# A trunk kernel's recurrence stage: a temporary in another buffer, a scaling on another engine

## The chip, the cores and the metric

The kernel runs on one NeuronCore of a Trainium2 chip. The metric is the time of one execution on the device in microseconds. Five engines work side by side, each through its own list of instructions in order: TensorE (PE) multiplies, VectorE (DVE) and ScalarE (ACT) work element by element, GpSimd (POOL) does small steps, SyncE (SP) issues the loads of weights. They wait for each other by semaphores. SBUF is the memory on the core, PSUM the small one into which PE writes.

## What is computed

One layer of a trunk: x is 512 frames of 1024 channels, in float32. The part that matters here is the second of its two branches, a gated linear recurrence of 8 heads, and how it is normed and gated:

```python
def reference(x, w_in, ...):
    h = rmsnorm(x, norm_mix[l])
    proj = h @ w_in[l]
    zu, zv, zq, zf, zi, zo, g_a, g_b = jnp.split(proj, split_points, axis=-1)
    y_a = gmlp_branch(zu, zv, ...) @ w_up_a[l]
    y_b = hgrn2_branch(zq, zf, zi, zo, ..., hg_norm_g[l]) @ w_up_b[l]
    mix = jax.nn.sigmoid(g_a) * y_a + jax.nn.sigmoid(g_b) * y_b
    x = x + mix @ w_out[l]
    h = rmsnorm(x, norm_ffn[l])
    x = x + jnp.square(jax.nn.relu(h @ w_ff1[l])) @ w_ff2[l]
    return rmsnorm(x, final_norm)

def hgrn2_branch(zq, zf, zi, zo, lb, layer_idx, norm_g):
    log_f = jax.nn.log_sigmoid(zf32)
    k = jax.nn.sigmoid(-zf32)
    q = jax.nn.silu(zq)
    # S_t = diag(f_t) S_{t-1} + k_t v_t^T,  o_t = S_t^T q_t, per head
    o = hgrn2_chunkwise(q, k, zi, log_f)
    o = rmsnorm(o, norm_g) * jax.nn.silu(zo)     # norm over the 128 values of a head
    return o
```

## The kernel before

Frames and channels lie in tiles of 128 partitions. A float32 product is done as three matmuls: each operand is split into a high part H (the value rounded to the matmul's type, written by ACT, line 96) and a low part L (the rest, by DVE, line 97), and `mm3` (lines 120 to 122) adds H·H, H·L and L·H. Weights come in tiles of 128x1024 (`raw`, 4 buffers, loaded by SP); their split parts are WH and WL, 5 buffers each.

Two weight tiles for 256 channels are multiplied together by `seven`, a scheme of seven products in place of eight: it needs sums of the weight tiles, s1 to s4, in two tiles s12 and s34 (tag "S", 2 buffers, DVE, lines 148 to 156), which are split like any weight. Its products are named prodx and prodzy, its partial results u and u3. PE operands n1 to n4 are sums of frames prepared before.

The recurrence stage goes in four rounds of two heads. `gates_round` computes F, K and Q of a pair with `seven` (the query's silu by `fin_q`, with a temporary `sig` in pool pt). `hgrn_pair` then forms the scores within frames' cells: at each level b = 1, 2, 4, 8, 16, 32, 64 PE does many small matmuls (tile sp, line 455), DVE multiplies K and P by running products of F (T, `double`, line 481) and copies cells by a mask (line 488). `outputs` makes each head's result: transposes of K (pk, line 517), state products pst and st (lines 522 to 526), the outputs po in PSUM (lines 532 and 534), their squares summed by ACT (hjunk, line 536), rstd by two POOL steps (rs_h, rr_h, lines 226 and 228), and the scaled output o_n in SBUF by DVE (line 539), four tiles of 128 frames per head. po uses tag "hm", of which there are two buffers, so head h+1's po waits until the last buffer is read.

`gate_o(g)` computes the output gate of two heads: a projection acc, sg = sigmoid of it (ACT, line 555), sg = acc·sg and o_n = o_n·sg (DVE, lines 556 and 558). sg stands in a buffer of tag "S", the one of the sums. gate_o(0) to gate_o(2) follow rounds 1 to 3, gate_o(3) stands inside the merge gates that come after, which are eight further uses of `seven` (ga, and F, Q, V, K of the name "4"; their sigmoids on line 171).

At the end `onto_channels` transposes o_n (py, line 586), and ACT and DVE write it times the norm's weights hng as operands ybH and ybL (lines 588 and 589) for the projection with the weights "upb" (acc, lines 120 to 122 with 512 columns).

The order of instructions on each engine is not the order of the code: a scheduler with a cost model of its own places the whole program, subject to the buffers. So an edit to a buffer or an engine moves instructions on all engines around it.

Of the kernel before, what the change touches and what calls it, by code (L numbers as in the profile page):

```python
# [8 lines left out]
F32 = mybir.dt.float32  # L9
F32R = mybir.dt.float32r  # L10
I32 = mybir.dt.int32
AF = mybir.ActivationFunctionType
ALU = mybir.AluOpType
AX = mybir.AxisListType

P = 128
S = 512
# [56 lines left out]
def trunk_kernel(ctx: ExitStack, tc: tile.TileContext, A: dict, out: bass.AP):  # L74
    nc = tc.nc
# [4 lines left out]
    wp = ctx.enter_context(tc.tile_pool(name="wp", bufs=1))  # L80
# [140 lines left out]
    hng = cst.tile([P, 1], F32, name="hng")  # L221
# [37 lines left out]
    o_n = pr.tile([P, NT, D], F32, name="o_n")  # L259
# [102 lines left out]
    for t in range(NT):  # L362
# [4 lines left out]
        r = rstd_of(gp, mv[:, 1:2], 1, EPS, "l")  # L367
# [45 lines left out]
    pt = left3.enter_context(tc.tile_pool(name="pt", bufs=1, side="left", reuse_waits="tile"))  # L413
    left2 = ExitStack()
    hg = left2.enter_context(tc.tile_pool(name="hg", bufs=1, side="left", reuse_waits="tile"))
    ps_sc = left3.enter_context(tc.tile_pool(name="ps_sc", bufs=1, space=bass.MemoryType.PSUM))
    nc.sync.dma_start(hng, A["hg_norm_g"].rearrange("o v -> v o"))
    mask = {}
    for b in (0, *LEVELS):
        mask[b] = hg.tile([P, 16 if b else C], I32, name=f"mask{b}")  # L420
# [7 lines left out]
    def gates_round(r, V):  # L428
        F, K, Q = (held(n, r) for n in "FKQ")

        def fin_f(i, cols, src):
            nc.scalar.activation(K[:, i, cols], src, AF.Sigmoid, scale=1.0 if i else -1.0)
            nc.scalar.activation(F[:, i, cols], src, AF.Sigmoid, scale=-1.0 if i else 1.0)  # L433

        def fin_q(i, cols, src):
            qc = Q[:, i, cols]
            sig = pt.tile([P, S], F32, tag="sig", bufs=1, name="sig")[:, cols]
            nc.scalar.activation(sig, src, AF.Sigmoid, scale=-1.0 if i else 1.0)
            nc.vector.scalar_tensor_tensor(qc, src, -1.0 if i else 1.0, sig, ALU.mult, ALU.mult)

        for z, g, fin in ((ZF, F, fin_f), (ZQ, Q, fin_q)):
            seven(("chan", z + 256 * r), ("chan", z + 256 * r + 128), rhs, pt, ps_sc, g, fin, True)
        return V, F, K, Q

    def hgrn_pair(r, V, F, K, Q0):
        def flat(x):
            return x.rearrange("p h t -> p (h t)")

        def cellwise(sp, x, n, of=1):

            for h in range(2):
                for t in range(NT):
                    for p in range(0, NC, of):
                        c0 = t * P + p * C
                        nc.tensor.matmul(sp[p * C:(p + 1) * C, (h * NT + t) * n:(h * NT + t + 1) * n],  # L455
                                         K[:, h, c0:c0 + C], x(h, c0), start=True, stop=True)

        def bank(name):
            return ps_sc.tile([P, S], F32, tag="sp", bufs=2, name=f"sp{r}_{name}")


        sp = bank(0)
        cellwise(sp, lambda h, c0: Q0[:, h, c0:c0 + C], C)
        Q = held("P", r)
        nc.vector.tensor_tensor(flat(Q), flat(Q0), flat(F), ALU.mult)
        nc.vector.copy_predicated(cl.rearrange("p h t c -> p (h t) c"),
                                  mask[0][:, None, :].broadcast_to([P, 2 * NT, C]),
                                  sp[:, :2 * NT * C].rearrange("p (n c) -> p n c", c=C))


        T = flat(F)

        def double(b, T):

            n = 2 * S // (2 * b)
            T2 = T.rearrange("p (g i) -> p g i", i=2)
            Tn = hg.tile([P, n], F32, tag=f"T{b}", bufs=1, name=f"T{b}_{r}")
            nc.vector.tensor_tensor(Tn, T2[:, :, 0], T2[:, :, 1], ALU.mult)
            for x, i in ((K, 0), (Q, 1)):
                xv = flat(x).rearrange("p (g i b) -> p g i b", i=2, b=b)[:, :, i, :]  # L480
                nc.vector.tensor_tensor(xv, xv, T2[:, :, 1 - i, None].broadcast_to([P, n, b]), ALU.mult)
            return Tn

        for b in LEVELS:
            sp = bank(b)
            cellwise(sp, lambda h, c0: Q[:, h, c0:c0 + C].rearrange("p (g i b) -> p g i b", i=2, b=b)[:, :, 1, :], 16)
            T = double(b, T)
            nc.vector.copy_predicated(
                cl.rearrange("p h t (g i b) -> p (h t) g i b", i=2, b=b)[:, :, :, 1, :],
                mask[b][:, None, :].broadcast_to([P, 2 * NT, 16]).rearrange("p n (g b) -> p n g b", b=b),  # L490
                sp[:, :2 * NT * 16].rearrange("p (n g b) -> p n g b", n=2 * NT, b=b))
        for p in range(NC):
            nc.scalar.copy(sc[p * C:(p + 1) * C, :, :, p * C:(p + 1) * C], cl[p * C:(p + 1) * C])

        sp = bank(C)
        cellwise(sp, lambda h, c0: Q[:, h, c0 + C:c0 + 2 * C], C, 2)
        for p in range(0, NC, 2):
            nc.scalar.copy(sc[p * C:(p + 1) * C, :, :, (p + 1) * C:(p + 2) * C],
                           sp[p * C:(p + 1) * C, :2 * NT * C].rearrange("p (h t c) -> p h t c", h=2, t=NT))
        T = double(C, T)  # L500

        sp = bank(64)
        for h in range(2):
            for t in range(NT):
                nc.tensor.matmul(sp[0:64, (h * NT + t) * 64:(h * NT + t + 1) * 64], K[:, h, t * P:t * P + 64],
                                 Q[:, h, t * P + 64:(t + 1) * P], start=True, stop=True)
        nc.scalar.copy(sc[0:64, :, :, 64:128], sp[0:64].rearrange("p (h t c) -> p h t c", h=2, t=NT))
        T = double(64, T)
        for h in range(2):
            outputs(2 * r + h, V, K[:, h, :], Q[:, h, :], sc[:, h], T[:, h * NT:(h + 1) * NT])  # L510

    def outputs(h, V, K, Q, sc, Tt):
        hc = slice((h % 2) * P, (h % 2 + 1) * P)

        pk = ps.tile([P, NT, P], F32, tag="hm", bufs=2, name=f"pk{h}")
        for t in range(NT - 1):
            nc.tensor.transpose(pk[:, t, :], K[:, t * P:(t + 1) * P], ident)
        kd = hg.tile([P, NT - 1, P], F32, tag="kd", bufs=1, name=f"kd{h}")
        nc.scalar.copy(kd, pk[:, :NT - 1, :])
        pst = ps.tile([P, NT, P], F32, tag="hm", bufs=2, name=f"pst{h}")  # L520
        for t in range(NT - 1):
            nc.tensor.matmul(pst[:, t, :], kd[:, t, :], V[:, t, hc], start=True, stop=True)
        st = hg.tile([P, NT - 1, P], F32, tag="st", bufs=1, name=f"st{h}")
        nc.vector.tensor_copy(st[:, 0, :], pst[:, 0, :])
        for t in range(1, NT - 1):
            nc.vector.scalar_tensor_tensor(st[:, t, :], st[:, t - 1, :], Tt[:, t:t + 1], pst[:, t, :],
                                           ALU.mult, ALU.add)
        po = ps.tile([P, NT, P], F32, tag="hm", bufs=2, name=f"po{h}")
        ssq = hg.tile([P, NT], F32, tag="hssq", bufs=2, name=f"hssq{h}")
        junk = hg.tile([P, P], F32, tag="hjunk", bufs=2, name="hjunk")  # L530
        for t in range(NT):
            nc.tensor.matmul(po[:, t, :], sc[:, t, :], V[:, t, hc], start=True, stop=t == 0)
            if t:
                nc.tensor.matmul(po[:, t, :], Q[:, t * P:(t + 1) * P], st[:, t - 1, :],
                                 start=False, stop=True)
            nc.scalar.activation(junk, po[:, t, :], AF.Square, accum_out=ssq[:, t:t + 1])
        r = rstd_of(hg, ssq, NT, P * EPS, "h")
        for t in range(NT):
            nc.vector.tensor_scalar(o_n[:, t, h * P:(h + 1) * P], po[:, t, :], r[:, t:t + 1], P ** 0.5,
                                    ALU.mult, ALU.mult)  # L540

    def merge_gate(c0, d, g):
        seven(("chan", c0 + 128 * d), ("chan", c0 + 128 * d + 128), rhs, pt, ps_sc, g, act_by_sign(g, AF.Sigmoid), True)
# [7 lines left out]

    def gate_o(g):
        def evac_zo(tp, acc):
            sg = wp.tile([P, S], F32, tag="S", bufs=2, name="sg").rearrange("p (j c) -> p j c", j=2)
            nc.scalar.activation(sg, acc, AF.Sigmoid)
            nc.vector.tensor_tensor(sg, acc, sg, ALU.mult)
            ov = o_n[:, 2 * tp:2 * tp + 2, g * 256:(g + 1) * 256]
            nc.vector.tensor_tensor(ov, ov, sg, ALU.mult)

        tok_proj(ZO + 256 * g, evac_zo)  # L560
# [69 lines left out]
    for hf in range(2):  # L630
        W = [wload("out", hf, k) for k in range(4)]
        cs = slice(hf * 512, (hf + 1) * 512)
        for t in range(NT):
# [4 lines left out]
            junk = pn.tile([P, S], F32, tag="junk", bufs=1, name="junk")  # L638
# [56 lines left out]
    for t in range(NT):  # L695
        for hf in range(2):
            for f in range(NSLOW - 2, NSLOW):
                ff2(f, t, hf)
            c = x2[:, t, hf * S:(hf + 1) * S]
# [195 lines left out]
```

## Time and profile before

| what | value |
|---|---|
| three runs | 842.28, 842.15, 840.13 us, median 842.15 |
| profiled execution | 840.37 us |
| its span | 838.4 us |
| granted TensorE clock, mean | 0.985 |
| PE busy | 815.2 us (97%) |
| DVE busy | 607.4 us (72%) |
| ACT busy | 421.4 us (50%) |
| POOL busy | 50.6 us (6%) |

The span runs from the first to the last instruction of the profiled execution; its own time is 1.97 us longer. "Granted clock" is the share of full speed at which PE was allowed to run in a stretch; 1.00 stands for 2.4 GHz and 0.50 for 1.2 GHz. PE's busy time is that of instructions, at either speed. An idle time is put down to the instruction whose end released the waiting one.

### The profile page before, as it was taken

The numbers are of one execution on the slowest core, as the hardware profiler recorded it, in microseconds if no ns is written. First come the engines' busy times: TensorE is split into PE (matmuls) and PEld (weight loads), VectorE is DVE, ScalarE is ACT, GpSimd is POOL, SyncE is SP. The second block draws the span as 40 slices with busy tenths as digits, with TensorE's granted clock in tenths as the row PEclk, the third lists the DMA queues.
The fourth block names the chain that finished last, engine by engine and source line by source line (L and its number), as shares of the span: only waits on it lengthen the run. The fifth ranks groups of instructions, "written<-read, shape, count | busy, mean of one in ns | idle before, by whom it ended". The sixth has DMA issues, their size and how long they took to land.

```text
span 838.4 us, 16623 instructions
## 1 busy us (share of the span) xinstructions
PE 815.2 (97%) x7026; PEld 744.9 (89%) x7026; DVE 607.4 (72%) x829; ACT 421.4 (50%) x688; POOL 50.6 (6%) x79
## 2 busy tenths in 40 slices
PE   8999999989999999998999999999999999999996
PEld 7989899988999989998888889999999988778884
DVE  7775377946778589947565359887777575899996
ACT  6624364526437246544533332777767552555464
POOL 2010000000010100100000012000000000010103
PEclk9999999998999999998999999999999999999998
DMA  8242142311224013332533412233333396193812
GB/s 322 77 150 77 29 124 59 98 52 37 92 77 126 3 52 113 94 97 76 151 99 112 176 59 84 76 104 120 105 102 101 107 301 179 33 293 98 220 26 100
DMA packets 27212, 92.29 MB, mean 110 GB/s; under 512 B 4161, under 2 KB 4161, under 8 KB 27138
## 3 DMA queue, kind: packets, MB, share of 16 engines
q1 hardware_dynamic: 24834, 83.89, 31.1%
q0 software_dynamic: 1728, 6.29, 4.1%
q8 instruction: 55, 0.90, 0.4%
q10 hardware_dynamic: 576, 1.05, 0.3%
q14 instruction: 19, 0.16, 0.1%
HBM read 89.13 MB, written 2.10 MB: 109 GB/s over the span
## 4 chain that ended last, share of the span: by engine, by line
PE 92%; ACT 2%; DVE 2%; issue 1%; DMA 1%; POOL 1%; SPq 0%; POOLq 0%; ACTq 0%; DVEq 0%
PE acc L120 11%; PE acc L121 11%; PE acc L122 11%; PE prodx L120 7%; PE prodx L122 7%; PE prodx L121 7%; PE prodzy L120 5%; PE prodzy L122 5%; PE prodzy L121 5%; PE hm L121 3%; PE hm L120 3%; PE hm L122 3%; PE y L121 2%; PE y L120 2%; PE y L122 2%; PE sp L455 2%
## 5 line engine op out<-in xcount | busy, mean ns | idle before, releaser
L97 DVE TENSOR_TENSOR WL<-raw,WH 128x1024 fp32r<-128x1024 f32 (+1 forms) x134 | 147.3, 1104 | 87.9 <-ACT WH L96 87.3
L96 ACT ACTIVATE WH<-raw 128x1024 fp32r<-128x1024 f32 (+1 forms) x134 | 128.6, 963 | 141.3 <-PE prodx L121 29.2
L120 PE MATMUL acc<-WH,hTH 128*128 128x256 f32 x320 | 91.7, 287 | 1.1 <-ACT F L433 1.1
L122 PE MATMUL acc<-WH,hTL 128*128 128x256 f32 x320 | 90.8, 284 | 0.0
L121 PE MATMUL acc<-WL,hTH 128*128 128x256 f32 x320 | 90.3, 283 | 0.0
L97 DVE TENSOR_TENSOR WL<-s,WH 128x1024 fp32r<-128x1024 f32 x60 | 73.3, 1223 | 22.5 <-ACT WH L96 21.6
L96 ACT ACTIVATE WH<-s 128x1024 fp32r<-128x1024 f32 x60 | 63.6, 1061 | 40.1 <-PE prodzy L121 9.2
L120 PEld LDWEIGHTS acc<-WH,hTH 128*128 128x128 f32 x320 | 60.3, 189 | 1.7 <-ACT F L433 1.4
L121 PEld LDWEIGHTS acc<-WL,hTH 128*128 128x128 f32 x320 | 60.3, 188 | 0.1
L122 PEld LDWEIGHTS acc<-WH,hTL 128*128 128x128 f32 x320 | 60.3, 189 | 0.0
L121 PE MATMUL hm<-WL,aH 128*128 128x512 f32 x96 | 38.1, 397 | 0.0
L122 PE MATMUL hm<-WH,aL 128*128 128x512 f32 x96 | 38.0, 396 | 0.0
L120 PE MATMUL hm<-WH,aH 128*128 128x512 f32 x96 | 37.9, 397 | 0.0
L120 PE MATMUL prodzy<-n1H,WH 128*128 128x256 f32 x120 | 34.5, 288 | 2.6 <-ACT WH L96 2.6
L120 PE MATMUL prodzy<-hTH,WH 128*128 128x256 f32 x128 | 36.3, 283 | 0.0
L121 PE MATMUL prodzy<-hTL,WH 128*128 128x256 f32 x128 | 36.1, 282 | 0.0
L122 PE MATMUL prodzy<-hTH,WL 128*128 128x256 f32 x128 | 36.1, 282 | 0.0
L122 PE MATMUL prodzy<-n1H,WL 128*128 128x256 f32 x120 | 34.3, 286 | 1.7 <-DVE WL L97 1.7
L120 PE MATMUL prodx<-n2H,WH 128*128 128x256 f32 x120 | 34.4, 286 | 0.7 <-ACT u L147 0.7
L120 PE MATMUL prodx<-n4H,WH 128*128 128x256 f32 x120 | 34.0, 284 | 0.5 <-DVE K L160 0.5
L96 ACT ACTIVATE WH<-rawx 128x1024 fp32r<-128x1024 f32 x24 | 25.1, 1053 | 18.7 <-issue 10.7
L122 PE MATMUL prodx<-n2H,WL 128*128 128x256 f32 x120 | 34.4, 287 | 0.0
(312 smaller groups left out, 2511.1 us busy)
## 6 DMA issues: line engine op xcount, KB each, us to landing
raw<-in_w_dram SPq DMA_DIRECT2D x128, 512.0 KB, 3.6
rawx<-in_w_dram SPq DMA_DIRECT2D x18, 512.0 KB, 7.9
rawx<-in_w_dram POOLq DMA_DIRECT2D x6, 512.0 KB, 7.0
raw<-in_w_dram POOLq DMA_DIRECT2D x6, 512.0 KB, 8.7
part<-in_x_dram SPq DMA_DIRECT2D x4, 512.0 KB, 5.8
x<-in_x_dram SPq DMA_DIRECT2D x4, 512.0 KB, 7.7
out_dram<-x ACTq DMA_DIRECT2D x4, 256.0 KB, 2.7
out_dram<-x SPq DMA_DIRECT2D x4, 256.0 KB, 2.5
```

The lines of the kernel that those rows point to most:

```text
L96: nc.scalar.activation(H, src, AF.Copy)
L97: nc.vector.tensor_tensor(L, src, H.bitcast(F32), ALU.subtract)
L120: nc.tensor.matmul(acc, ah, bh, start=first and i == 0, stop=False, **kw)
L121: nc.tensor.matmul(acc, ah, bl, start=False, stop=False, **kw)
L122: nc.tensor.matmul(acc, al, bh, start=False, stop=last and i == n - 1, **kw)
L455: nc.tensor.matmul(sp[p * C:(p + 1) * C, (h * NT + t) * n:(h * NT + t + 1) * n], K[:, h, c0:c0 + C], x(h, c0), start=True, stop=True)
```

## The change

Five edits, all in the recurrence stage:

- sg of `gate_o` is taken from pool pt, tag "sig", with two buffers, which it shares with `fin_q`'s temporary; before it had a buffer of the sums' tag "S".
- o_n is written by ACT (a copy with a scale per row) and no longer by DVE.
- The factor root of 128, which DVE multiplied in with the scale, is multiplied into hng by one POOL instruction after hng is loaded.
- The products T of the levels share two buffers by turns, where each level had one of its own.
- The squares' junk tile has one buffer for two.

```diff
@@ hng is loaded
     nc.sync.dma_start(hng, A["hg_norm_g"].rearrange("o v -> v o"))
+    nc.gpsimd.tensor_scalar(hng, hng, P ** 0.5, None, ALU.mult)
@@ fin_q
-            sig = pt.tile([P, S], F32, tag="sig", bufs=1, name="sig")[:, cols]
+            sig = pt.tile([P, S], F32, tag="sig", bufs=2, name="sig")[:, cols]
@@ double
-            Tn = hg.tile([P, n], F32, tag=f"T{b}", bufs=1, name=f"T{b}_{r}")
+            Tn = hg.tile([P, S], F32, tag="Ta", bufs=1, name=f"T{b}_{r}") if b in (1, 4, 16, 64) else \
+                hg.tile([P, S // 2], F32, tag="Tb", bufs=1, name=f"T{b}_{r}")
+            Tn = Tn[:, :n]
@@ outputs
-        junk = hg.tile([P, P], F32, tag="hjunk", bufs=2, name="hjunk")
+        junk = hg.tile([P, P], F32, tag="hjunk", bufs=1, name="hjunk")
@@ outputs, after rstd
         for t in range(NT):
-            nc.vector.tensor_scalar(o_n[:, t, h * P:(h + 1) * P], po[:, t, :], r[:, t:t + 1], P ** 0.5,
-                                    ALU.mult, ALU.mult)
+            nc.scalar.activation(o_n[:, t, h * P:(h + 1) * P], po[:, t, :], AF.Copy, scale=r[:, t:t + 1])
@@ gate_o
-            sg = wp.tile([P, S], F32, tag="S", bufs=2, name="sg").rearrange("p (j c) -> p j c", j=2)
+            sg = pt.tile([P, S], F32, tag="sig", bufs=2, name="sg").rearrange("p (j c) -> p j c", j=2)
```

The scheduler's new order, at three places. In the rows a name's number tells tiles of one name apart; those of the changed kernel are one higher, and its lines two or three.

PE in the first pair, around the outputs po of head 1 (po_1556 before, po_1557 now), before:

```order
L121 MATMUL prodzy<-hTL,WH 128x256
L122 MATMUL prodzy<-hTH,WL 128x256
L455 MATMUL sp_4_2059<-P_1980,K_1692 32x16 x32
L532 MATMUL po_1556<-V_703,scores 128x128 x2
L534 MATMUL po_1556<-st_1552,P_1272 128x128
L455 MATMUL sp_8_2097<-P_1980,K_1692 32x16 x24
L532 MATMUL po_1556<-V_703,scores 128x128
L534 MATMUL po_1556<-st_1552,P_1272 128x128
```

and now:

```order
L121 MATMUL acc<-WL,hTH 128x256
L456 MATMUL sp_2_2022<-P_1981,K_1693 32x16 x8
L535 MATMUL po_1557<-V_703,scores 128x128
L456 MATMUL sp_2_2022<-P_1981,K_1693 32x16 x24
L122 MATMUL acc<-WH,hTL 128x256
L120 MATMUL prodzy<-hTH,WH 128x256
L121 MATMUL prodzy<-hTL,WH 128x256
L122 MATMUL prodzy<-hTH,WL 128x256
L120 MATMUL prodzy<-hTH,WH 128x256
L121 MATMUL prodzy<-hTL,WH 128x256
L535 MATMUL po_1557<-V_703,scores 128x128
L537 MATMUL po_1557<-st_1553,P_1273 128x128
```

Head 1's outputs stand one level of the recurrence earlier, and products of 256 columns now stand between them; 24 products acc stand just ahead of this piece.

DVE at the last output gate, gate_o(3), where sums s0 and s1 of two merge gates are made, before (sg_4915 is the gate's second half):

```order
L148 TENSOR_TENSOR s0_4923<-raw57_4921 128x512
L556 TENSOR_TENSOR sg_4915<-acc_4866,sg_4915 128x512
L149 TENSOR_TENSOR s0_4923<-s0_4923,raw56_4919 128x512
L558 TENSOR_TENSOR o_n_77<-o_n_77,sg_4915 128x2x256
L155 TENSOR_TENSOR s1_4924<-raw56_4919,raw57_4921 128x512
L156 TENSOR_TENSOR s1_4924<-raw56_4919,s0_4923 128x512
L97 TENSOR_TENSOR WL_4949<-s0_4923,WH_4948 128x1024
L97 TENSOR_TENSOR WL_4993<-s1_4924,WH_4992 128x1024
```

and now (the same half is sg_4916, the sums s0_4924 and s1_4925):

```order
L156 TENSOR_TENSOR s1_4925<-raw56_4920,s0_4924 128x512
L163 TENSOR_TENSOR Q4_4555<-u_4688,prodzy_4687 128x512
L160 TENSOR_TENSOR Q4_4555<-prodx_4686,u3_4689 128x256
L97 TENSOR_TENSOR WL_4950<-s0_4924,WH_4949 128x1024
L148 TENSOR_TENSOR s0_5046<-raw59_5044 128x512
L149 TENSOR_TENSOR s0_5046<-s0_5046,raw58_5042 128x512
L97 TENSOR_TENSOR WL_4994<-s1_4925,WH_4993 128x1024
L558 TENSOR_TENSOR sg_4863<-acc_4814,sg_4863 128x512
L155 TENSOR_TENSOR s1_5047<-raw58_5042,raw59_5044 128x512
L156 TENSOR_TENSOR s1_5047<-raw58_5042,s0_5046 128x512
L560 TENSOR_TENSOR o_n_77<-o_n_77,sg_4863 128x2x256
L97 TENSOR_TENSOR WL_5026<-raw57_4922,WH_5025 128x512
```

The sums and their low parts stand ahead of both halves of the gate (the second half, sg_4916, follows this piece), and the next gate's sums s0_5046 and s1_5047 do too.

ACT where the merge gates end and the operands ybH of the projection "upb" begin, before:

```order
L96 ACTIVATE WH_5357<-raw63_5355 128x1024
L171 ACTIVATE K4_4556<-K4_4556 128x512
L171 ACTIVATE K4_4556<-K4_4556 128x256
L588 ACTIVATE ybH0_5168<-py_5170,hng_73 128x512
L588 ACTIVATE ybH1_5177<-py_5179,hng_73 128x512
L96 ACTIVATE WH_5392<-raw64_5390 128x1024
L171 ACTIVATE K4_4556<-prodx_5047 128x256
```

and now:

```order
L171 ACTIVATE K4_4557<-K4_4557 128x256
L96 ACTIVATE WH_5358<-raw63_5356 128x1024
L96 ACTIVATE WH_5393<-raw64_5391 128x1024
L171 ACTIVATE K4_4557<-prodx_5048 128x256
L171 ACTIVATE K4_4557<-K4_4557 128x512
L590 ACTIVATE ybH0_5169<-py_5171,hng_73 128x512
L590 ACTIVATE ybH1_5178<-py_5180,hng_73 128x512
```

The split of weight 64 and the sigmoid of the last product moved from behind ybH of heads 0 and 1 to ahead of them.

## Rows read from the trace of the kernel before

**Rows 1.** The page, part 1: engine, busy us (share of span) x instructions.

```profile
PE 815.2 (97%) x7026; PEld 744.9 (89%) x7026; DVE 607.4 (72%) x829; ACT 421.4 (50%) x688; POOL 50.6 (6%) x79
```

**Rows 2.** Waits of PE, 126 to 411 us: line waited for, total, times, longest.

```profile
PE prodzy L120 <- ACT WH L96: 2.6, 2, 1.8
PE prodzy L122 <- DVE WL L97: 1.7, 2, 1.2
PE po L532 <- DVE o_n L539: 1.3, 1, 1.3
PE acc L120 <- ACT F L433: 1.1, 1, 1.1
...
PE prodx L120 <- DVE K L160: 0.5, 1, 0.5
...
PE acc L120 <- ACT ybH L588: 0.3, 1, 0.3
PE py L586 <- DVE ybL L589: 0.3, 1, 0.3
PE prodx L120 <- ACT V L394: 0.2, 1, 0.2
```

**Rows 3.** Stretches of place A: length, busy time by engine, PEclk, DMA share, GB/s.

```profile
181.00:183.00 2.00, 1.15 (x68) 0.85 (x66) 1.53 (x6) 0.00 (x0) 1.34 (x2) 1.00 0.00 0
183.00:185.00 2.00, 0.90 (x4) 0.71 (x5) 2.00 (x7) 0.37 (x2) 0.00 (x0) 0.91 0.00 0
...
187.00:189.00 2.00, 1.83 (x23) 1.50 (x22) 0.87 (x2) 0.37 (x2) 0.00 (x0) 0.50 0.00 0
...
193.00:195.00 2.00, 2.00 (x55) 1.96 (x48) 1.47 (x3) 0.77 (x2) 0.00 (x0) 0.53 0.04 8
```

**Rows 4.** Timeline of POOL and DVE at 180 to 183 us: start, us, instruction.

```profile
180.47 0.54 POOL L226 TENSOR_SCALAR rs_h<-hssq 128x4 f32<-128x4 f32 x1 [78.34 <-ACT hjunk L536]
181.09 1.33 POOL L228 TENSOR_TENSOR rr_h<-rs_h,neghalf 128x4 f32<-128x4 f32 x1
...
182.46 1.13 DVE L539 TENSOR_SCALAR o_n<-po,rr_h 128x128 f32<-128x128 f32 x4 [0.47 <-POOL rr_h L228]
```

**Rows 5.** Place D: timeline of DVE and PE, and one stretch as in rows 3.

```profile
382.68 0.69 DVE L556 TENSOR_TENSOR sg<-acc,sg 128x512 f32<-128x512 f32 x1 [3.60 <-ACT sg L555]
383.29 0.68 DVE L149 TENSOR_TENSOR s<-s,raw 128x512 f32<-128x512 f32 x1
...
382.96 0.28 PE L121 MATMUL prodx<-hTL,WH 128*128 128x256 f32 x1
383.08 0.28 PE L122 MATMUL prodx<-hTH,WL 128*128 128x256 f32 x1
385.11 0.39 PE L120 MATMUL prodzy<-n1H,WH 128*128 128x256 f32 x1 [1.75 <-ACT WH L96]
...
387.09 0.58 PE L122 MATMUL prodzy<-n1H,WL 128*128 128x256 f32 x1 [1.24 <-DVE WL L97]
387.47 0.41 PE L120 MATMUL prodzy<-n1H,WH 128*128 128x256 f32 x1
...
392.80 0.31 PE L121 MATMUL prodzy<-hTL,WH 128*128 128x256 f32 x1
...
387.00:389.00 2.00, 1.91 (x9) 1.91 (x10) 1.95 (x4) 1.52 (x3) 0.00 (x0) 0.50 0.65 240
```

**Rows 6.** Squares of po by shape (busy, mean ns), and DVE's waits for rstd.

```profile
L536 ACT ACTIVATE hjunk<-po 128x128 f32<-128x128 f32 x32 | 8.8, 276 | 38.0 <-PE po L534 20.9 <-PE po L532 17.0
...
  POOL rr_h L228: 8.7, 7
```

**Rows 7.** Timeline of PE at 202 to 207 us: the groups sp and pk.

```profile
202.26 1.15 PE L505 MATMUL sp<-P,K 128*64 128x64 f32 x16
...
206.24 0.49 PE L517 MATMUL pk<-ident,K 128*128 128x128 f32 x3
```

**Rows 8.** Timeline of ACT and PE at 406 to 409 us.

```profile
406.27 1.06 ACT L96 ACTIVATE WH<-raw 128x1024 fp32r<-128x1024 f32 x1 [1.79 <-PE prodx L121]
...
408.79 0.49 PE L120 MATMUL acc<-ybH,WH 128*128 128x512 f32 x1 [0.30 <-ACT ybH L588]
```

**Rows 9.** Stretches at 528 to 536 us, columns as in rows 3.

```profile
528.00:530.00 2.00, 1.42 (x13) 1.22 (x11) 2.00 (x3) 2.00 (x3) 0.00 (x0) 1.00 0.00 0
530.00:532.00 2.00, 0.98 (x6) 0.78 (x7) 2.00 (x4) 2.00 (x6) 0.00 (x0) 1.00 0.64 233
...
534.00:536.00 2.00, 2.00 (x11) 2.00 (x10) 1.50 (x2) 0.76 (x3) 0.00 (x0) 0.50 0.36 55
```

## The prediction

> **What bounds the kernel now.** I read the page first: TensorE (PE) is busy 815.2 us of the 838.4 us span, VectorE (DVE) 607.4, ScalarE (ACT) 421.4 [rows 1]. So the kernel is PE's list of matmuls plus the places where PE stands, and an edit that touches no matmul can only change those places. Written out by engine, the two programs are the same up to the first recurrence pair (about 127 us of this trace) and again from the output projection on (about 411 us), and the weight loads go out in one order. So the second view is what PE waited for between 126 and 411 us [rows 2]; the reader is to see that a handful of waits holds everything. The third is the granted clock around the two largest: what a stall costs behind itself is seen there and not in the idle time. The last are the rows of the chains that end in those waits.
>
> Place A, 181 to 195 us: head 1's first output matmul waits 1.33 us for DVE's scaled outputs of head 0 (1.3 in [rows 2]). The chain is POOL's two steps for rstd, 0.54 and 1.33 us, then four DVE multiplies, 1.13 us [rows 4], and PE has little to do meanwhile. The granted clock then stands at 0.50, the 1.2 GHz level, until about 194.5 [rows 3]. Idle there are 0.85 us in 181 to 183, 1.10 in 183 to 185 and 0.17 in 187 to 189 [rows 3], 2.1 in all. Some 9.6 us of work ran at half clock. A 256-column matmul starts every 0.213 us at half clock (25 steps between the two PE rows of [rows 5], 5.33 us) and every 0.12 at full clock (the two PE rows ahead of them there). 9.6 x (1 - 0.12/0.213) = 4.2. A costs 6.3 us.
> Place D, 383 to 393 us: the gated output's temporary sg takes one of the two buffers of the weight sums. ACT's sigmoid and DVE's product at 382.68 must be done before the sum s at 383.29 [rows 5], and PE waits 1.75 us for the split WH of s and 1.24 for WL [rows 5]; then half clock to about 392.8 [rows 5]. 25 steps at 0.213 instead of 0.12 are 2.3 us: D costs 3.0 + 2.3 = 5.3.
> Place C, 301 to 305 us, is the same tie one gate earlier: what is left of the first two lines of [rows 2], 0.85 + 0.45 = 1.3 us; the clock stays up. Place B: 1.13 us for the gate F at 207. Place E, 406 to 410: 0.5 + 0.3 + 0.3 = 1.1 us for K, ybH and ybL [rows 2].
>
> **The change part by part.**
> *sg out of the sums' buffers.* The sums no longer wait for sigmoid and product. In the new order both sums of D stand ahead of the last sg pair on DVE, and C's no longer follow one. I take both places whole: -5.3 and -1.3. The new buffers, shared with the query's sigmoid, are two; a user holds one for an ACT and a DVE step of 0.6 to 0.7 us each (0.69 for the product [rows 5]), so the user two later finds it free. If that cover went, one such pair, 1.3, is the price.
> *Outputs scaled on ACT.* DVE loses 32 multiplies, 8 x 1.13 = 9.0 us [rows 4], nearly all beside PE work. ACT gains 32 operations that the trace does not show. The nearest row is the square of the same 128x128 tile in PSUM, 0.28 us [rows 6]: four end to end take 1.1, overlapped as DVE's are 0.8; for the scale that is read per row I allow up to 1.4. I take 1.0 for four, 8 us in all, on an engine that is half idle [rows 1]. What counts is order: ACT works in its order, and behind the four copies stand splits WH that PE needs. At most one such split stands close behind at any head, and there are five operand buffers ahead of it. I price it at zero, and rival 4 is the case where that is wrong.
> The Trainium skill, "ScalarE: Activation LUTs", speaks against the move: its section "Rules for kernel authors" gives a plain multiply to VectorE. Its section "What ACT_TABLE_LOAD costs" puts such an ACTIVATE at 186 + 93 (pointer scale) + 0.833 x 128 = 386 ns with 93 ns of overlap, an estimate of 1.27 us for four; by that figure each head's chain would be 0.3 us longer than in my sum. The rows of this case show less of a gap between the engines: 0.28 for one on ACT, 1.13 for four on DVE.
> *Root of 128 in the norm's weights.* One POOL operation on 128x1 after an early load; POOL is busy 6% [rows 1] and had been idle 78 us ahead of 180.47 [rows 4]. Zero. Were its cover gone, one POOL step, at most 1.33.
> *Two buffers for the products T, one for the squares' junk.* T's chain can no longer run ahead; each level of the recurrence waits for PE's cells in between anyway. Zero, at most one DVE step, 0.7. The squares already stand in one order on ACT.
> *What the new order does.* At A, between head 0's last and head 1's first output matmul PE now has 26 matmuls of the next projection, 3 of the state and 19 small ones, about 3.9 us, against a chain of 2.4 (last square and POOL) + 1.0; and two dozen large ones stand between the output matmuls. The 1.33 goes, and with it the reason for half clock. A wait for the copy V stays (0.2 in [rows 2]; 0.4 by my count, since it now follows head 1's last output). -6.3 + 0.4 = -5.9.
> At B a group sp of 64 columns, 1.15 us, stands ahead of the waiting projection instead of pk, 0.49 [rows 7]: -0.7.
> At the start of the first pair (about 150 us) a projection waits for gate F behind a split that itself waits for PE. That is B's wait again: between 0 and 1.13, taken 0.9 because the chain is the same. At the start of the third (about 209 us) a DVE sum stands behind a weight load that comes late: 0 to 1.24 (the longest wait for DVE's WL), taken 0.8.
> At E, a new cost. Before, ACT ran ybH for heads 0 and 1 and only then the split of the next weight. Now two splits, one of which waits for PE's last product of the merge gates, and K's two sigmoids stand ahead of ybH. One such split, the two sigmoids and ybH take 2.52 us in before, from 406.27 to PE's first matmul on ybH at 408.79 [rows 8], under 1.4 us of PE work. Now nothing covers them: PE idles about 2.5 instead of 1.1, +1.4. Does the clock fall? Idle of 0.58 and 1.02 us in 528 to 532 was followed by 0.50 in 534 to 536 [rows 9]; 1.13 at B brought none. 2.5 in one piece is nearer the former. Price: some 3.4 us of half clock there x 0.44 = 1.5; behind D some 6.9 x 0.44 = 3.0; I take 2.2.
> The sum: -5.9 - 0.7 - 1.3 - 5.3 + 0.9 + 0.8 + 1.4 + 2.2 = -7.9. The profiled execution took 840.37 us (the span and 1.97 around it): 832.5. The median of the three runs, 842.15, lies 1.8 above it; I put 0.5 of that on: **833.0 us**.
>
> **The rivals.**
> 1. E keeps its clock. For: B's 1.13 and C's scattered 1.3 did no harm. Against: 528 to 536. Time: 833.0 - 2.2 = 830.8.
> 2. One spell of half clock returns elsewhere. Several places in the new order have only 0.2 to 0.3 us to spare by my count (near 150, 328 and 377 us), and a late DVE or ACT there makes a wait like A's or D's. Price: 5.5, D's: 838.5.
> 3. Nothing comes of it. POOL's rstd ends each chain whatever engine follows, and DVE already sat 8.7 us in 7 times waiting for it [rows 6]. ACT takes that over: A's wait stays under another name (5.9 not gained), and the other seven heads add 0.4 each: 833 + 5.9 + 2.8 = 841.7.
> 4. Slower: ACT's queue behind rstd. A head's POOL steps (1.9 [rows 4]) and four copies (0.8 to 1.4) are some 3 us in which ACT may start no split. If PE's next split is due inside them, PE waits 1 to 1.5 and, as in A, half clock follows for 4. It decides where a WH that stands behind the copies is due less than 3 us plus a split (1.06 [rows 8]) after the last square. With three of eight heads so, 3 x 5 = 15: 848. Against it: ACT is half idle, five operands are buffered, and a split stands right behind the copies at few heads, where I count 0.5 to 1.0 us of room. The skill's rule above would push this way.
>
> **How the numbers follow.** Forecast 0.42, rival 1 0.20, rival 2 0.16, rival 3 0.10, rival 4 0.12. About 0.3% is what a measurement of this kernel can tell from no change, 839.6 to 844.7. Faster: 0.42 + 0.20 + 0.16, less 0.02 for rival 2's upper end = 0.76; same 0.10 + 0.02, less 0.01 for rival 3's upper end = 0.11; slower 0.13. The unknown terms (the two new waits 0 to 2.4 against 1.7, the clock 1.5 to 3.0, the copies) are worth 3 either way; with rivals 1 and 2 the range is 827.5 to 841, leaving out rival 4 and half of rival 3.
>
> **What would show it.** In the changed kernel's trace: clock 1.00 from 175 to 195 us and no PE wait over 0.5 on ACT's o_n; no wait of prodzy on WH or WL of a sum near either old place; PE idle about 2.5 us ahead of the first acc on ybH (near 400 us), then half clock for 3 to 7 us; ACT idle on POOL's rr_h at most heads, about 1 us each. Wrong would be a PE wait on a WH that stands behind the copies, half clock anywhere else in 127 to 395 us, or E under 1.5 us.

## The result and the profile after

| kernel | median, us | lowest to highest | ratio to before, 95% interval |
|---|---|---|---|
| before | 841.14 | 839.05 to 842.28 (4 runs) | |
| changed | 827.81 | 825.89 to 830.50 (4 runs) | 0.9847 [0.9806, 0.9887] |
| changed, measured again | 828.83 | 826.43 to 830.34 (6 runs) | 0.9870 [0.9847, 0.9892] |

The change made the kernel faster by 12 to 13 us; 833.0 had been forecast. In its second measurement the kernel before had a median of 840.63 us. The profiled execution of the changed kernel took 830.50 us, the longest of its four runs, with a span of 828.4.

The page of the changed kernel, part 1, engines as in [rows 1]:

```profile
PE 809.9 (98%) x7026; PEld 740.8 (89%) x7026; DVE 597.6 (72%) x797; ACT 429.7 (52%) x720; POOL 49.4 (6%) x80
```

PE's busy time fell from 815.2 to 809.9 us with the same 7026 matmuls: in the main, that is work that no longer runs at half clock. VectorE (DVE) lost 9.8 us, ScalarE (ACT) gained 8.3, as the scaling's move asks.

What PE waited for in the changed kernel up to the projection "upb" (126 to 401 us), as in [rows 2]:

```profile
PE acc L120 <- ACT ybH L590: 2.4, 1, 2.4
PE acc L120 <- ACT F L434: 1.3, 2, 0.7
PE prodx L120 <- ACT V L394: 0.5, 1, 0.5
PE po L537 <- DVE st L527: 0.3, 1, 0.3
```

The waits of places A, C and D (po on o_n, prodzy on WH and WL) are gone from the list. What is new is 2.4 us on ybH, place E.

Place A in the changed kernel, stretches as in [rows 3], and the rows of the chain (POOL, ACT, then PE's first output matmul of head 1):

```profile
181.00:183.00 2.00, 2.00 (x74) 1.69 (x73) 1.54 (x3) 0.84 (x4) 0.00 (x0) 1.00 0.03 8
183.00:185.00 2.00, 2.00 (x19) 2.00 (x19) 2.00 (x4) 1.22 (x3) 0.00 (x0) 1.00 0.73 231
187.00:189.00 2.00, 1.55 (x63) 1.33 (x51) 1.47 (x4) 1.39 (x5) 0.00 (x0) 1.00 0.52 199
```

```profile
178.24 1.33 POOL L228 TENSOR_TENSOR rr_h<-rs_h,neghalf 128x4 f32<-128x4 f32 x1
...
179.60 1.14 ACT L542 ACTIVATE o_n<-po,rr_h 128x128 f32<-128x128 f32 x4 [2.14 <-POOL rr_h L228]
...
181.41 0.49 PE L535 MATMUL po<-V,scores 128*128 128x128 f32 x2
```

The chain is as long as it was in [rows 4]: 1.33 us on POOL and 1.14 for the four scalings, now ACT's. But PE is busy through all of it, the output matmul finds its tile ready, and the clock stays at 1.00. The 0.45 idle at 187 to 189 is the wait for the copy V.

Place D, DVE's rows and one stretch:

```profile
361.91 0.68 DVE L149 TENSOR_TENSOR s<-s,raw 128x512 f32<-128x512 f32 x1
...
364.78 0.68 DVE L156 TENSOR_TENSOR s<-raw,s 128x512 f32<-128x512 f32 x1
...
378.81 0.69 DVE L558 TENSOR_TENSOR sg<-acc,sg 128x512 f32<-128x512 f32 x1 [0.65 <-ACT sg L557]
...
381.00:383.00 2.00, 2.00 (x20) 2.00 (x18) 1.35 (x2) 0.97 (x1) 0.00 (x0) 1.00 0.29 88
```

Both sums of the place, s0 (line 149) and s1 (line 156), now end more than 13 us ahead of the product of the second sg at 378.81, where in [rows 5] s0 came behind it; PE has no wait there.

Place E, ACT's chain, PE's first matmul on ybH and three stretches:

```profile
396.64 1.06 ACT L96 ACTIVATE WH<-raw 128x1024 fp32r<-128x1024 f32 x1 [0.34 <-PE prodx L121]
397.60 0.37 ACT L171 ACTIVATE K<-prodx 128x256 f32<-128x256 f32 x1
397.87 0.62 ACT L171 ACTIVATE K<-K 128x512 f32<-128x512 f32 x1
398.39 1.26 ACT L590 ACTIVATE ybH<-py,hng 128x512 fp32r<-128x512 f32 x2
...
399.12 1.18 PE L120 MATMUL acc<-ybH,WH 128*128 128x512 f32 x2 [2.44 <-ACT ybH L590]
...
397.00:399.00 2.00, 0.00 (x0) 0.00 (x0) 1.98 (x2) 2.00 (x5) 0.00 (x0) 1.00 0.78 231
399.00:401.00 2.00, 1.88 (x7) 1.55 (x8) 1.41 (x2) 0.64 (x2) 0.00 (x0) 0.55 0.87 209
401.00:403.00 2.00, 2.00 (x7) 1.59 (x7) 0.75 (x1) 0.69 (x1) 0.00 (x0) 0.60 0.93 332
```

A split WH, K's two sigmoids and ybH follow one another for 2.4 us, and PE has nothing else. In this execution the clock stood at 0.50 from 399.2 to 402.6.

To compare kernels without the parts that no edit touches, I use the time from the first matmul acc on yaH (ahead of the recurrence) to the first on mixH (behind the projection "upb"). Rows of these tiles in before, then in the changed kernel: count, duration min/median/max, first and last start:

```profile
L120 PE MATMUL acc<-yaH,WH x32: 389/395/398, 77.1 to 100.2; 128*128 128x512 f32 x32
...
L120 PE MATMUL acc<-WH,mixH x64: 389/389/476, 456.3 to 501.0; 128*128 128x512 f32 x64
```

```profile
L120 PE MATMUL acc<-yaH,WH x32: 389/395/398, 79.6 to 102.7; 128*128 128x512 f32 x32
...
L120 PE MATMUL acc<-WH,mixH x64: 389/389/476, 447.7 to 492.4; 128*128 128x512 f32 x64
```

Before took 456.3 - 77.1 = 379.2 us, the changed kernel 447.7 - 79.6 = 368.1. The changed kernel came 2.5 us later to this stretch, in code that the change does not touch; the other kernels below came to it at 77.0 to 78.0, but for one (79.7).

### The profile page after: what moved, and what is told of

It is laid out like the page before. It is cut to its first block, busy times and chain, and to the rows that moved or that the text cites. A ratio compares the mean times of both kernels' runs of the same rounds, so it can differ in the third digit from the quotient of the medians.

```text
span 828.4 us, 16602 instructions
## 1 busy us (share of the span) xinstructions
PE 809.9 (98%) x7026; PEld 740.8 (89%) x7026; DVE 597.6 (72%) x797; ACT 429.7 (52%) x720; POOL 49.4 (6%) x80
## 4 chain that ended last, share of the span: by engine, by line
PE 93%; ACT 2%; DVE 2%; DMA 1%; issue 1%; POOL 0%; SPq 0%; POOLq 0%; ACTq 0%; DVEq 0%
PE acc L120 12%; PE acc L121 11%; PE acc L122 11%; PE prodx L120 7%; PE prodx L121 7%; PE prodx L122 7%; PE prodzy L120 5%; PE prodzy L122 5%; PE prodzy L121 5%; PE hm L121 3%; PE hm L120 3%; PE hm L122 3%; PE sp L456 2%; PE y L122 2%; PE y L120 2%; PE y L121 2%
## 5 line engine op out<-in xcount | busy, mean ns | idle before, releaser
L121 PE MATMUL prodx<-n4L,WH 128*128 128x256 f32 x120 | 33.8, 281 | 0.0
```

Source lines behind the costliest of these rows:

```text
L121: nc.tensor.matmul(acc, ah, bl, start=False, stop=False, **kw)
```

## The experiments

The theory when they began: place A went because of the order into which the shared T buffers force the recurrence, C and D because of sg's new buffer, and the scaling on ACT brought nothing but E. The rival is one that the prediction had left open: that A's relief is tied to the scaling on ACT and the order around it. The table of what came out stands at the end of this section.

**The scaling alone.** The kernel before with:

```diff
+    nc.gpsimd.tensor_scalar(hng, hng, P ** 0.5, None, ALU.mult)
-            nc.vector.tensor_scalar(o_n[:, t, h * P:(h + 1) * P], po[:, t, :], r[:, t:t + 1], P ** 0.5,
-                                    ALU.mult, ALU.mult)
+            nc.scalar.activation(o_n[:, t, h * P:(h + 1) * P], po[:, t, :], AF.Copy, scale=r[:, t:t + 1])
```

> The kernel before with only the scaling of the outputs on ScalarE and the root of 128 in the norm's weights. Written out, PE's order at head 1's first output matmul stays as before (32 small matmuls ahead, two output matmuls in a row), the sums at gate 3 still stand behind sg, and ybH keeps its early place. Theory (place A went by the reordering that the shared T buffers brought): A, C and D all stay, 838 to 842, with a PE wait of 1 to 2 us on po near 183 us and half clock behind it. Rival (A went because ScalarE took the scaling over): A gone, 834 to 836, clock 1.00 from 181 to 195.

841.39 us against 840.54, ratio 1.0022 [1.0000, 1.0044]: no gain. PE's waits, two rows of ACT and three stretches:

```profile
PE prodzy L120 <- ACT WH L96: 3.5, 2, 1.8
PE prodzy L122 <- DVE WL L97: 2.5, 2, 1.2
PE prodx L120 <- ACT u L154: 2.4, 1, 2.4
PE po L533 <- ACT hjunk L537: 1.3, 2, 1.0
PE prodx L120 <- ACT u L147: 1.1, 1, 1.1
...
190.76 1.14 ACT L540 ACTIVATE o_n<-po,rr_h 128x128 f32<-128x128 f32 x4 [1.48 <-POOL rr_h L228]
191.77 1.07 ACT L96 ACTIVATE WH<-s 128x1024 fp32r<-128x1024 f32 x1
...
183.00:185.00 2.00, 0.89 (x28) 0.60 (x18) 1.85 (x5) 1.40 (x6) 0.33 (x1) 1.00 0.00 0
187.00:189.00 2.00, 1.20 (x14) 0.95 (x8) 1.50 (x3) 1.39 (x5) 0.00 (x0) 1.00 0.01 4
...
201.00:203.00 2.00, 2.00 (x12) 2.00 (x10) 1.26 (x3) 0.88 (x2) 0.00 (x0) 0.52 0.00 0
```

Head 1's output matmuls still wait, 1.0 us and 0.3, now for the square that stands behind the scalings on ACT. But the half clock that the theory had named behind them did not come: the clock stayed at 1.00 until 199.5 us, which was the rival's sign. So the scaling by itself does change A; the time goes elsewhere. The fourth rival of the prediction shows itself: o_n of head 1, which waited for rstd, stands ahead of the split of a sum, WH at 191.77, and holds it by about 1.5 us (by my count its sum and its bank were ready by 190.2). A wait of 1.1 us for u follows, and along the chain from there, over WL, K, the cells and a copy on ACT, one of 2.4 us with the clock at 0.52 behind it. C and D stay (the first two rows hold 6.0 us for both, 3.0 each), so C's waits are 3.0 us here and not 1.3, with half clock from 305.3 to 312.1. The rival theory is out by its time, 834 to 836.

**The T buffers and the junk buffer alone.**

```diff
-            Tn = hg.tile([P, n], F32, tag=f"T{b}", bufs=1, name=f"T{b}_{r}")
+            Tn = hg.tile([P, S], F32, tag="Ta", bufs=1, name=f"T{b}_{r}") if b in (1, 4, 16, 64) else \
+                hg.tile([P, S // 2], F32, tag="Tb", bufs=1, name=f"T{b}_{r}")
+            Tn = Tn[:, :n]
-        junk = hg.tile([P, P], F32, tag="hjunk", bufs=2, name="hjunk")
+        junk = hg.tile([P, P], F32, tag="hjunk", bufs=1, name="hjunk")
```

> The kernel before with only the two T buffers and the single junk buffer. In the written order large matmuls now stand ahead of and between head 1's output matmuls; sg still shares the sums' buffers. Theory: A gone by itself, about -6: 834 to 836, C and D as before, with half clock near 380 to 392. Rival (A went by ScalarE): A stays in some form and the time is 839 to 842; the shared buffers alone cost or give nothing.

833.62 us, ratio 0.9919 [0.9890, 0.9948]. PE's waits, two stretches at A and one at D:

```profile
PE prodzy L120 <- ACT WH L96: 2.6, 2, 1.8
PE prodzy L122 <- DVE WL L97: 1.7, 2, 1.2
...
179.00:181.00 2.00, 2.00 (x19) 2.00 (x18) 2.00 (x6) 1.21 (x2) 0.00 (x0) 1.00 0.00 0
181.00:183.00 2.00, 2.00 (x19) 1.96 (x17) 1.95 (x4) 0.72 (x3) 0.00 (x0) 1.00 0.22 33
...
384.00:386.00 2.00, 2.00 (x12) 2.00 (x10) 2.00 (x4) 0.37 (x1) 0.00 (x0) 0.50 0.20 23
```

A is gone with the scaling still on DVE: PE is busy and the clock 1.00. C and D have the very waits of [rows 2]. Behind D the clock stood at 0.50 from 383.0 to 386.4, 3.4 us, where in before it did so from 386.0 to 392.8, 6.8 us. No run takes the junk buffer apart from the T buffers; the next one leaves it as it was.

**T's order without the shared buffers.** A buffer that is shared can only add waits; so is it the order? Every T keeps its own buffer, and each is only queued on DVE behind the last reader of the T two levels back:

```diff
-            nc.vector.tensor_tensor(Tn, T2[:, :, 0], T2[:, :, 1], ALU.mult)
+            t = nc.vector.tensor_tensor(Tn, T2[:, :, 0], T2[:, :, 1], ALU.mult).ins
+            for i in readers.get(b in (1, 4, 16, 64), ()):
+                tc.add_manual_dep(t, i.name, mybir.DependencyInfo(mybir.DependencyClass.NoSync,
+                                                                  mybir.DependencyReason.DATA), reason="order")
...
```

> The kernel before with every T in its own buffer, but DVE's order held as two buffers would hold it: each T queued behind the last reader of the T two levels back (order of issue, no wait). 22 large matmuls stand ahead of head 1's first output matmul and 7 between the first two. Theory (A goes because the paced order gives PE work between the heads, not because of the buffers or of ScalarE): A's wait of po under 0.5, no half clock at 181 to 195, D and C as before: 833 to 837. Rival (the buffers themselves matter, or the order was luck): a po wait of 1 us and half clock: 839 to 843.

833.31 us, ratio 0.9920 [0.9893, 0.9946]. PE's waits and a stretch at A:

```profile
PE prodzy L120 <- ACT WH L96: 3.6, 2, 1.9
PE prodzy L122 <- DVE WL L97: 3.1, 2, 1.8
PE po L540 <- ACT hjunk L544: 0.5, 1, 0.5
...
181.00:183.00 2.00, 2.00 (x76) 1.84 (x75) 2.00 (x5) 1.65 (x5) 0.00 (x0) 1.00 0.00 0
```

The same gain with the buffers of before, the junk buffers too. A is full of work; a wait of 0.5 for the square is left. C and D stay, and C is larger here than in before (the first two rows hold 6.7 us for both places against 4.3 in [rows 2]).

**T buffers and sg, scaling on DVE.** The changed kernel with the first diff of this section undone.

> The changed kernel with the scaling put back on DVE (and the root of 128 back into it). In the written order A and D are as in the changed kernel, and ybH of heads 0 and 1 stands ahead of the split of weight 64, as before. Theory (ScalarE's part brings nothing but place E's longer wait): no 2.4 us wait at the first acc on ybH, no half clock behind it, 824 to 827, not slower than the changed kernel. Rival (the scaling on ScalarE relieves A): a wait of po on o_n of 1 us or more and half clock near 180 to 195, 832 to 835.

826.27 us, ratio 0.9838 [0.9805, 0.9871], and once more beside the changed kernel:

> The changed kernel with the scaling on DVE once more, beside the changed kernel on one chip. Theory (ScalarE's part costs place E and brings nothing): 1 to 3 us below the changed kernel, 825 to 827. Rival (the difference seen before was spread): equal within 0.7 us.

826.23 us, ratio 0.9834 [0.9811, 0.9857], where the changed kernel had 828.83, 0.9870 [0.9847, 0.9892], on the same chip. PE's waits:

```profile
PE acc L120 <- ACT F L433: 1.3, 2, 0.7
...
PE acc L120 <- ACT ybH L590: 0.3, 1, 0.3
```

Against the T buffers alone sg's move is worth 833.62 - 826.27 = 7.4 us. C and D are gone, and so is E's long wait: in this kernel's order ybH stands ahead of the split of weight 64. The scaling on ACT is no part of the gain: the kernel without it has the lower median, by 2.6 us on the same chip, though the intervals overlap by a little.

**T buffers and the scaling, sg with the sums.** The changed kernel with sg's two lines undone.

> The changed kernel with sg back in the sums' buffers: T buffers and the scaling on ScalarE. ybH stands ahead of the split of weight 64 here. Theory (the scaling's engine is worth nothing by itself once PE has work between the heads; C and D are sg's): within 2 us of the kernel with the buffers alone, 831 to 836, C and D waits as in the kernel before, no 2.4 us wait for ybH. Rival (ScalarE helps beside the order): 829 to 831; other rival (it hurts, splits behind rstd): 837 or more with PE waits on WH at the heads.

836.75 us, ratio 0.9952 [0.9931, 0.9974]. PE's waits and a stretch behind C:

```profile
PE prodzy L120 <- ACT WH L96: 3.6, 2, 1.8
PE prodzy L122 <- DVE WL L97: 3.0, 2, 1.7
...
301.00:303.00 2.00, 2.00 (x10) 2.00 (x11) 2.00 (x4) 2.00 (x3) 0.00 (x0) 0.50 0.57 229
```

C and D together are 6.6 us of waits, and behind C the clock now stands at 0.50. The time came 0.75 us over the theory's band and 3.1 above the kernel with the buffers alone, though the two were measured on different chips and their intervals overlap. D's waits are the old ones (3.0), and there is no long one for ybH; but C's are 3.6 us where the theory had them as in before (1.3), and its half clock lasted from 299.5 to 306.3. Of the second rival neither the time came (837 or more) nor the sign, a wait on a split behind rstd.

**ybH ahead.** The changed kernel with the last merge gate's sigmoids issued behind ybH of heads 0 and 1 on ACT, and the splits of the weights "upb" from the fifth on queued behind them:

```diff
+    with tc.issue_after(ybi[1]):
+        for f in late:
+            f()
...
+        if d >= 4:
+            with tc.issue_after(ybi[1]):
+                UB = wload("upb", d)
```

> The changed kernel with ybH of heads 0 and 1 ahead of the last merge gate's sigmoids and ahead of the split of weight 64 on ScalarE. The order is the changed kernel's up to there; in the feed-forward part some products change places. Theory (E's wait and the clock behind it cost what they show): the wait at the first acc on ybH falls from 2.4 to 0.5 or less, no half clock at 399 to 403, 823 to 826. Rival (the wait only moves, to ybL or to the second acc): 827 to 829, with the same idle time summed over the 4 us after.

825.94 us, ratio 0.9834 [0.9802, 0.9866]. The two waits of PE at E:

```profile
395.02 0.50 PE L120 MATMUL acc<-ybH,WH 128*128 128x512 f32 x1 [0.25 <-ACT ybH L597]
...
396.66 0.66 PE L595 MATMUL py<-ident,o_n 128*128 128x128 f32 x4 [1.13 <-DVE ybL L598]
```

The 2.44 us became 0.25, and a part of it, 1.13, moved to ybL. With E mended, the kernel with the scaling on ACT is level with the one that scales on DVE (826.27): what the scaling's move costs in the changed kernel is E's order. In the kernels where sg stays with the sums it came with a larger C instead.

**Filling E.** The changed kernel with matmuls of the identity into a bank of their own, 20 of them, between the merge gates and acc:

```diff
+    with tc.issue_after(last):
+        for i in range(20):
+            filled = nc.tensor.matmul(fill[:, i % NT, :], ident, ident, start=True, stop=True).ins
...
+        with tc.issue_after(filled):
+            mm3(acc, [(blk(UB, k), yb[k]) for k in range(KD)])
```

> The changed kernel with 20 matmuls of the identity, whose result nobody reads, between the merge gates' last product and the first acc on ybH: PE works through about 2 us of the 2.4 us wait. Theory (half clock follows PE's idle time): wait at acc on ybH under 0.6, clock 1.00 from 396 to 405, and the time 0 to 2 us below the changed kernel, 825 to 828. Rival (the clock falls there for something else, or fillers don't hold it): half clock at 399 to 403 again and 827.5 to 830.

828.46 us, ratio 0.9871 [0.9847, 0.9895]. There was no half clock from 396 to 405, as the theory had it, but the time lay above its band. I had taken a filler, one such matmul, at half its price:

```profile
394.30 4.73 PE L587 MATMUL fill<-ident 128*128 128x128 f32 x40
```

They ran 2 us past the wait. So 10 of them:

> The changed kernel with 10 of the identity matmuls ahead of the first acc on ybH; 20 of them took 4.73 us and ran 2 us past the end of ybH, so 10 take about 2.3 and should end with it. Theory (half clock behind E costs the changed kernel about 1.3 us, in the executions where it comes): clock 1.00 from 394 to 404 in the profile, PE's wait there under 0.5, median 826 to 827.5, so 1 to 2 below the changed kernel's 828. Rival (the clock behind E matters little and the spread has other sources): the same median as the changed kernel, 828 to 829.

829.84 us, ratio 0.9869 [0.9840, 0.9898]. PE's rows (10 fillers are 20 records) and a stretch behind them:

```profile
396.61 2.50 PE L587 MATMUL fill<-ident 128*128 128x128 f32 x20
...
400.00:402.00 2.00, 2.00 (x15) 1.69 (x13) 1.11 (x2) 0.69 (x1) 0.00 (x0) 1.00 0.71 283
```

The wait is full, the clock 1.00, and the median is no lower than the changed kernel's 828.83 and 827.81; the ratio to before on its own chip is level with the changed kernel's too (0.9869 and 0.9870). By the medians the rival holds. But the profile shows that they can't settle it: this execution came to the stretch 2 us late (79.7 us), and half clock came behind the idle time at the start of the feed-forward part (521.9 to 525.3 us). Both lie outside of E and hide what half clock there costs. A second profile of the changed kernel shows that cost.

**The changed kernel again.**

> The changed kernel once more, for its spread and a second profile. Theory (the wait for ybH is in the program, the fall of the clock behind it happens in part of the executions): 2.4 us wait at the first acc on ybH again; half clock behind it or not; runs from 825.5 to 830.5, median 827 to 829. Rival (the clock falls every time, or never again): the wait with half clock in each, all runs at 828 to 831, or all at 825 to 826.5.

828.83 us. PE's first matmul on ybH and the stretch behind it:

```profile
396.70 0.50 PE L120 MATMUL acc<-ybH,WH 128*128 128x512 f32 x1 [2.44 <-ACT ybH L590]
...
397.00:399.00 2.00, 1.94 (x11) 1.34 (x10) 1.18 (x3) 0.91 (x2) 0.00 (x0) 1.00 0.84 262
```

The same wait of 2.44 us, and the clock stayed at 1.00. From the first acc on ybH to the first on mixH it took 444.0 - 396.7 = 47.3 us, where the first profile, with half clock, took 447.7 - 399.1 = 48.6: the fall costs 1.3 us when it comes. How often it comes stays open. Of the changed kernel's ten runs three had a mean clock of 0.997 and took 825.89 to 826.43 us, six had 0.994 and took 828.06 to 830.50; where their half clock lay only the two profiles show.

**ybL ahead, scaling on DVE.** The kernel with T buffers and sg, with the splits of weights "upb" from the fourth on queued behind ybH of head 1.

> The kernel with T buffers and sg but the scaling on DVE, and the split of weights 63 and 64 queued behind ybH of head 1 on ScalarE, so that DVE makes ybL of heads 0 and 1 first. Theory (the two waits of 0.3 us on ybH and ybL are what is left at E beside 0.5 for K): both gone, 0.3 to 0.8 us below that kernel, 825 to 826. Rival (the two weights are late instead, a wait of acc on WH or WL of 0.5 us or more): 826 to 828.

825.45 us, ratio 0.9823 [0.9795, 0.9850]. The waits on ybH and ybL are gone, but the stretch is 365.3 us as without the edit (365.4 and 365.3): a wait of 0.4 for the query appeared in the new order at 271 us. Not told apart from the kernel without the edit.

All of them, by the stretch from yaH to mixH of their profiles:

| kernel | places left | stretch, us | median, us |
|---|---|---|---|
| before | A, C, D | 379.2 | 841.14 |
| scaling alone | A (its waits), C, D | 381.1 | 841.39 |
| T buffers alone | C, D | 372.7 | 833.62 |
| T order alone | C, D | 374.4 | 833.31 |
| T buffers and scaling | C, D | 375.1 | 836.75 |
| changed | E | 368.1, again 366.5 | 827.81, again 828.83 |
| changed, E filled with 20 | E filled | 368.4 | 828.46 |
| changed, E filled with 10 | E filled | 366.6 | 829.84 |
| changed, ybH ahead | none of them | 365.6 | 825.94 |
| T buffers and sg | none of them | 365.4, again 365.3 | 826.27, again 826.23 |
| the same, ybL ahead | none of them | 365.3 | 825.45 |

## Why the prediction was right, and where not

The sign was right. The time of 827.81 lies only 0.3 us inside the low end of the range (827.5), and that it lies inside is luck: single runs of the changed kernel go from 825.89 to 830.50. By its steps:

- **Place A.** Nearly right in size: 5.9 + 0.7 forecast for A and B, and 379.2 - 372.7 = 6.5 in the stretch of the T buffers alone, but about 1.0 of that came at D, where PE worked for 5.8 us at half clock in before and for 3.4 there (2.4 x 0.44). That leaves 5.5. Right that PE would be busy through the chain and the clock stay up. The step that failed stands under "Two buffers for the products T": "Zero, at most one DVE step". The T buffers, priced at nothing, bring A's gain by themselves, through the order that they force. I gave it to "what the new order does" without asking which edit made the order; the order of each edit by itself would have answered that.
- **Outputs scaled on ACT.** Priced at zero for PE, and so it is: level with DVE when E is mended. Four scalings took 1.14 us on ACT and 1.13 on DVE. The estimate from the Trainium skill ("ScalarE: Activation LUTs", section "What ACT_TABLE_LOAD costs"), 386 ns for one, is close to the trace's 368 (median of 32 in the changed kernel), and its 1.27 for four is 0.13 above. The rule of the same page of the Trainium skill (section "Rules for kernel authors") that a multiply belongs on VectorE shows no cost here: 825.94 us with the scaling on ACT and E mended, 826.27 with it on DVE.

```profile
L542 ACT ACTIVATE o_n<-po,rr_h x32: 359/368/386, 179.6 to 351.5; 128x128 f32<-128x128 f32 x32
```

- **Places C and D.** 1.3 + 5.3 = 6.6 forecast, 7.4 between the medians with and without sg's move. The nearness is in part luck. In the kernel with the T buffers alone C and D held 1.3 + 3.0 us of waits and 3.4 us of half clock, worth 1.5 at 0.44: 5.8; no row of PE's waits or of its clock shows the rest. In the kernel before C had 0.5 us more of idle time, at 307 to 309, which the forecast left out. And C is no fixed price: in three kernels with another order it held 3.0 to 3.7 us of waits, and 6.8 of half clock. The one after the same two waits of D, 3.0 us, lasted 6.8 us in before and 3.4 in the four other kernels that had them.
- **Place B and the two new waits.** The two waits for F of the changed kernel are 0.7, at the first pair's start (0.9 forecast), and 0.6, at B (1.1 - 0.7 = 0.4 forecast); the third pair's start cost 0.3 against 0.8. Together about 0.5 less than the sum had.
- **Place E.** The wait was forecast at 2.5 and is 2.44 in both profiles, from a chain of four rows of before that another order had hidden. The term behind it was too large: 2.2 for half clock, where the fall costs 1.3 and came in one of two profiles. Rival 1 (E keeps its clock, 830.8) and the forecast both occur, from one execution to the next.
- **The sum.** -7.9 forecast for the profiled execution; the stretch gave 379.2 - 368.1 = 11.1, with half clock at E as forecast. Of the 3.2 between, C's idle time is 0.5, the waits of B and the starts 0.5, the clock at E 0.9, and the two spells at A and D 0.3: I counted 9.6 and 25 x 0.213 = 5.3 us of work in them, where PE was busy for 9.8 and 5.8 us of the 10.2 and 6.8 at 0.50. No row here accounts for the last 1.0.
- **What the profile should show.** The clock of 1.00 from 175 to 195, no wait on o_n, no wait on a sum's split, 2.4 us at E and 3 us of half clock behind it: all there. "ACT idle on POOL's rr_h": 8.0 us in 6 times.

Rival 4, ACT's queue behind rstd, did not happen in the changed kernel, but it is real: in the kernel with the scaling alone a split behind o_n brought a wait of 2.4 us. The order around the copies differs between the two; no run separates that from the other edits.

The profiled execution came 2.0 us below its forecast (830.50 against 832.5), the median 5.2 below its own (827.81 against 833.0). The difference has a part which no term was made for: what differs between executions of one program. The changed kernel's first profile began the stretch at 79.6 us, the second at 77.5, and the idle time at 517 to 523 us, where before fell to half clock [rows 9], did not bring it in either profile of the changed kernel. Each of the two is worth about 1.5 to 2 us, and the late start worked against the gain.

## What to carry to other kernels

Where a scheduler places the program, an edit to a buffer is an edit to the order: take the edits apart and write out the order that each one makes before giving any of them a price. A buffer that paces a chain on one engine can be worth more than the engine that the change moves work to, because it leaves other engines' work between two dependent steps. And a temporary that shares a buffer with operands' sums puts a sigmoid and a product into the path of a weight: look for it wherever PE waits for a split.

## What was not expected of the hardware

The clock's fall is not a function of the wait alone. The same 2.44 us wait at E was followed by 0.50 in one profile of the changed kernel and by 1.00 in the other. At the start of the feed-forward part, in code that no kernel here changed, PE idles about 1.6 us within 3 us in all thirteen profiles; the clock fell behind it in five of them and not in eight. Two waits of 3.0 us in sum, as at D, were followed by half clock every time, in all five profiles that had D, but for 6.8 us in one of them and 3.4 in the other four. A single execution's profile therefore carries 1 to 3 us that belong to no edit, and a term for half clock behind a wait of this size is a chance, not a price.
